# A first-FFN product placed one place earlier, two kinds of input sums formed while x arrives, and six instead of four splits of h ahead of the last silu

## The chip, the cores and the metric

The kernel runs on one core of a Trainium2 chip. TensorE multiplies, ScalarE and VectorE prepare its operands and handle its results, GpSimd and SyncE issue transfers (queues named POOL and SP in the profile). The metric is the device time of one execution in microseconds (us), median of several runs; lower is better.

## The reference

One hybrid encoder block in float32 on x of 512 tokens by 1024 features:

```
x = x + 1/2 * (silu(g1) * u1) @ W1_down,   [g1|u1] = rmsnorm(x) @ W1_gu     (5632 columns)
h = rmsnorm(x);  y = gated RG-LRU branch(h) + gated neighbourhood attention(h)
x = x + y @ W_out
x = x + 1/2 * (silu(g2) * u2) @ W2_down,   [g2|u2] = rmsnorm(x) @ W2_gu
```

The change is in the two FFNs, which share their code. Each has 22 feature tiles of 128 for its h = silu(g) * u.

## The kernel before

**Numbers in two parts.** TensorE takes operands in a reduced float32 format (`F32R`). So each operand is split into a high part H (ScalarE copies it with rounding, line 140) and a low part L (VectorE subtracts, line 143), and each matmul is done three times: high by high, low by high, high by low. In the profile the tiles are `wh`, `wl` for weights, `xh`, `xl` for x, `hh`, `hl` for h.

**Four products' worth of output from seven.** For 20 of the 22 tiles the up projection is done in five *units* of four feature tiles by `strassen`. The 512 tokens and 1024 input features are each halved, which gives x the quarters a11, a12, a22 and the sums s1, s2, s4, s3 (`FORMS`, made by `make_forms`). A unit multiplies seven of these with four weight blocks a_, b_, c_, d_ and sums of them. Each product is two halves of the contraction (`kp`) and has 24 matmuls of 128 by 512; a half needs one split weight. In unit one the order is a11, a12, s1, s2, s4, s3; the seventh, a22 (`last_product`), is done in the next unit, between s1 and s2. Results leave the banks by `evict` (ScalarE), by `plus` (VectorE adds them to an earlier result), and by `gate` and `put` (silu, scaling, a transpose, and a transfer of h to memory by `flush`). Sums of weights are made by accumulating transfers (`add`, POOL's queue) or by VectorE (`sums`).

**Sums of x.** `raw` makes the sum of one quarter pair on VectorE (lines 273 to 280), s2 from s1 and s4 from s2; `cut` rounds a pair of them to high and low parts. In the first FFN both are called when a product needs them (`need`, line 487), in the second all sums are made ahead.

**The start.** In the first FFN, x and the weights of two `plain` feature tiles arrive in eight steps; each step splits one tile of x and of the weights, squares x for the norm, keeps a scaled copy xg, and multiplies into four banks of `aux`, evicted as `pre`. In the second FFN the two plain tiles are ordinary products.

**The turn.** After the units, `finish` (line 557) fetches the turned h of unit one back (`fetch`, eight transfers on POOL's queue, four for each half of the tokens), loads three down weights and calls `ahead`, which splits h tiles by `cut`; before tile 2 it fetches unit two as well. Then `last_put` does the last silu. The down projection runs over the 22 h tiles, adding into all eight banks.

**What sets the order.** The program is written in one sequence; a planner orders each engine's instructions ahead of time. An instruction whose inputs it expects to be there goes in the order of the program, those under `high_priority` ahead of all others. Each engine then works through its list in order and waits where an input is late. Tiles carry a tag with a number of buffers: `big` 42 (sums, parts, evictions, s, h), `wh` and `wl` 4 each (split weights), `pair` 4, `PT` 5 (weights c_, d_, turned h), `wraw` 3, and 4 banks each for `acc` and `aux`. `hold` places a transfer behind a given matmul; `keep_in_program_order` fixes the order of the first loads.

Of the kernel before, what the change touches and what calls it, by code (L numbers as in the profile page):

```python
# [19 lines left out]
KT = D // P  # L20
# [19 lines left out]
C_G1, C_GM, C_G2 = 0, 8, 16  # L40
# [11 lines left out]
DFIRST = 3  # L52
# [34 lines left out]
def block_kernel(ctx: ExitStack, tc, a, out):  # L87
# [15 lines left out]
    def nm(s):  # L103
        uid[0] += 1
        return f"{s}_{uid[0]}"
# [9 lines left out]
    def acc_t():  # L115
        return acc.tile([P, T], F32, tag="acc", name=nm("acc"))

    def aux_t():
        return aux.tile([P, T], F32, tag="aux", name=nm("aux"))
# [140 lines left out]
    FORMS = "s1", "s2", "s4", "s3"  # L260
# [28 lines left out]
    def four_k(tag, bufs):  # L289
        return big.tile([P, 1024], F32, tag=tag, bufs=bufs, name=nm(tag))  # L290

    def strassen(src, units, A, norm, hd, need, ready, finish):

        half = T // 2
        prev, out, state_, rc = {}, [], {}, []

        def raws(u, i, tag, bufs):
            ts = []
            for kp in range(2):
                t = four_k(tag, bufs) if tag != "wraw" else raw_t()  # L300
                ld = nc.sync.dma_start(t, src[u, i, kp])
                if u == 0 and nld[0] < 8:
                    tc.keep_in_program_order(ld)
                ts.append(t)
            return ts

        def product(pss, ws, form, first, last, out_now=True):
            for kp in range(2):
                H, L = ws[kp]() if callable(ws[kp]) else ws[kp]
                for k2 in range(2):  # L310
                    k = kp * 2 + k2
                    c = slice(k2 * T, (k2 + 1) * T)
                    xh_, xl_ = A[form][k]
                    for tb in range(2):
                        s = slice(tb * P, (tb + 1) * P)
                        for x_, w_ in ((xh_, H), (xl_, H), (xh_, L)):
                            mark["mm"] = nc.tensor.matmul(  # L317
                                pss[tb], x_[:, s], w_[:, c], start=first and k == 0 and x_ is xh_ and w_ is H,
                                stop=k == 3 and w_ is L, skip_group_check=True)
            if out_now:  # L320
                flush()

        def operand(raw):
            w = hl_t()
            with nullcontext() if state_["u"] == 0 else tc.high_priority():
                split(raw, *w)
            return w

        def operands(ts):
            return [lambda t=t: operand(t) for t in ts]  # L330

        def add(u, ts, i):
            with tc.high_priority():
                for kp, t in enumerate(ts):
                    nc.gpsimd.dma_start(t, src[u, i, kp], accum_op=ALU.add)

        def sums(ts, os):
            def one(t, o):
                with tc.high_priority():
                    nc.vector.tensor_tensor(t, t, o, ALU.add)  # L340
                return operand(t)
            return [lambda t=t, o=o: one(t, o) for t, o in zip(ts, os)]

        def evict(pss, n):
            ts = [big_t(n=n) for _ in pss]
            with tc.high_priority():
                for t, ps in zip(ts, pss):
                    nc.scalar.activation(t, ps, AF.Copy)
            return ts

        def plus(ts, pss):
            for t, ps in zip(ts, pss):
                nc.vector.tensor_tensor(t, t, ps, ALU.add)

        def gate(ts, th):
            ss = [big_t(n="s") for _ in ts]
            for tb, (s_, t) in enumerate(zip(ss, ts)):
                j = th * 2 + tb
                nc.scalar.activation(s_, t, AF.Silu, scale=rc[0][:, j : j + 1])
            return ss  # L360

        def flush(q=nc.sync):
            while out:
                to, t2 = out.pop(0)
                hold(q.dma_start(to, t2))

        def put(u, ss, ts, th):
            for tb, (s_, t) in enumerate(zip(ss, ts)):
                j = th * 2 + tb
                mark["h"] = nc.vector.scalar_tensor_tensor(t, t, rc[0][:, j : j + 1], s_, ALU.mult, ALU.mult)  # L370
                t2 = big_t(n="ht")
                nc.vector.transpose(
                    t2.rearrange("p (c f i) -> p f c i", c=NCB, i=32), t.rearrange("p (f c i) -> p f c i", c=NCB, i=32))
                out.append((hd[u][j], t2.rearrange("p (c x) -> p c x", c=NCB)))

        def last_product(p, out_now=True):
            product(p["Z"], operands(p["a"]), "a22", False, True, out_now)

        def last_put(p):
            put(p["u"], gate(p["Z"], 1), p["u7"], 1)  # L380

        for u in range(units):
            state_["u"] = u
            a_ = raws(u, 0, "pair", 4)
            c_ = raws(u, 2, "PT", 5)
            d_ = raws(u, 1, "PT", 5)
            b_ = raws(u, 3, "wraw", 3)
            Z = [acc_t() for _ in range(2)]
            product(Z, operands(a_), "a11", True, False)
            p1 = evict(Z, "p1")  # L390
            if u == 0:
                add(u, a_, 1)
            if u == 0:
                rc.append(norm())
            if u == units - 1:
                need("plain")
            Y = [acc_t() if u == 0 else aux_t() for _ in range(2)]
            product(Y, operands(c_), "a12", True, True)
            if u == 0:
                need("s1")  # L400
            plus(p1, Y)
            if u > 0:
                s1 = gate(p1, 0)
            X = [aux_t() for _ in range(2)]
            w = operands(a_) if u == 0 else sums(a_, d_)
            product(X, w, "s1", True, False)
            add(u, d_, 3)
            p5 = evict(X, "p5")
            if prev:
                last_product(prev)  # L410
                last_put(prev)
            w = sums(a_, b_)
            if u == 0:
                need("s2")
            product(Z, w, "s2", False, False)
            add(u, a_, 2)
            u2 = evict(Z, "u2")
            if u == 0:
                need("s4")
            product(X, operands(b_), "s4", False, True)  # L420
            if u == 0:
                need("s3")
                ready(rc[0])
                s1 = gate(p1, 0)
            plus(u2, X)
            put(u, s1, u2, 0)
            product(Z, operands(d_), "s3", False, False, u < units - 1)
            plus(p5, Z)
            prev = dict(u=u, Z=Z, u7=p5, a=a_)
        last_product(prev, False)  # L430
        finish()
        last_put(prev)
        flush(nc.gpsimd)

    def ffn(wgu, ws, wd, xh, xl, forms, ssum, plain, res, emit_out, lead=None, end=None):
        units = (FT - plain) // 4
        half = T // 2
        hd = [dram.tile([NCB, P, NCB, P], F32, tag="hd", bufs=12, name=nm("hd")) for _ in range(units)]
# [27 lines left out]
        else:  # L466
            r = None
            for m in range(plain):
                pg, pu = acc_t(), acc_t()
                feat_chunk(wgu[2 * m], KT, xh, xl, pg, 0, KT)  # L470
                if r is None:
                    r, rcol, _ = rstd(ssum)
# [22 lines left out]
        def ready(rc):  # L495
# [4 lines left out]
            for tb, t in enumerate(toks):  # L500
# [8 lines left out]
        A = {"a11": quarter(0, slice(0, half)), "a12": quarter(4, slice(0, half)),  # L509
             "a22": quarter(4, slice(half, T))}  # L510
# [33 lines left out]
        def ahead(n):  # L544
            while len(cuts) < min(n, FT):
                k = len(cuts)
                if k >= plain and (k - plain) % NCB == 0:
                    u = (k - plain) // NCB
                    if u + 1 < units:
                        fetch(u + 1)  # L550
                cut(k)
# [5 lines left out]
        def finish():  # L557
            fetch(0)
            for k in first:
                ws_[k] = load_w(wd[k], 1024)  # L560
            ahead(DFIRST + 1)

        strassen(ws, units, A, norm, hd, need, ready, finish)

        def put_in(m, k, last=FT - 1):
            H, L = ws_[k]
# [92 lines left out]
    class Forms:  # L659
# [5 lines left out]

        def tile(self, k):
            self.xg.append(scaled(self.gcol, k))
            if k >= KT // 2 and self.eager:
                for n in FORMS:
                    self.raw(n, k - KT // 2)  # L670

        def cut(self, n):
            if not self.eager:
                for k in range(len(self.S[n]), len(self.S[n]) + 2):
                    self.raw(n, k)
            self.cut_(n)
# [2 lines left out]
            for n in FORMS:  # L679
                self.cut(n)  # L680

    forms = Forms(C_G1, False)

    def lead_step(k):
        square(k)
# [173 lines left out]
    A = [None] * KT  # L859
# [256 lines left out]
    for hf in range(2):  # L1116
        st = tiny.tile([P, 2, NCB, 8], F32, tag="st", name=nm("st"))
        raws = [qk_raw(0, hf, st), qk_raw(1, hf, st)]
# [42 lines left out]

    nxt = {}
    load_pairs()
    forms = Forms(C_G2, True)
    for m in range(KT):
        nc.sync.dma_start(xres[m], xd[m])
        ps = acc_t()
# [101 lines left out]
```

## Time and profile before

| | |
|---|---|
| median of 3 runs | 1106.3 us (1103.4 to 1107.08) |
| profiled execution, its own time | 1102.27 us |
| its span, first to last instruction | 1100.5 us |
| TensorE busy | 1082.4 us, 98% |
| VectorE, ScalarE, GpSimd busy | 70%, 51%, 18% |
| mean granted TensorE clock | 0.995 |

A row of the timeline has the start in us, the length in us, engine, line, operation, output<-inputs, shapes, how many instructions are merged in it, and in brackets how long the engine had been idle and what ended that. PE is TensorE, DVE VectorE, ACT ScalarE. A row of the waits has the total, how often, and the longest. A letter q behind an engine is its queue of transfers. Lines are those of the kernel before.

### The profile page before, as it was taken

What the parts mean: (1) busy time and instruction counts of PE and PEld (TensorE: products, weight loads), DVE (VectorE), ACT (ScalarE), POOL (GpSimd) and SP (SyncE); (2) the same over time, 40 slices, a digit from 0 to 9 for tenths busy, and PEclk for the clock granted to TensorE, in tenths of its full rate; (3) what the DMA queues carried; (4) which work ended last, traced back from release to release, by engine and by line L of the source; (5) the groups of instructions that cost most, each with busy time, mean ns of one, the idle gap of its engine ahead of it and who ended that gap; (6) DMA issues with size and microseconds to landing.
All of it is one profiled execution on the core that took longest, in us unless ns stands there. A gap on an engine that the chain in (4) does not pass through costs nothing. (4 is left out here: it accounts for less than half of the span.)

```text
span 1100.5 us, 14411 instructions
## 1 busy us (share of the span) xinstructions
PE 1082.4 (98%) x5121; PEld 885.4 (80%) x5121; DVE 771.3 (70%) x1222; ACT 561.6 (51%) x866; POOL 197.7 (18%) x340
## 2 busy tenths in 40 slices
PE   9899999999999999999999999999999999999998
PEld 7778888878888778788787788888888888878887
DVE  6887788774426786899878896768677887773422
ACT  7655555543314668776544543356455554543310
POOL 0101002432000333132325322000000001323000
PEclk9999999999999999999999999999999999999999
DMA  9957767785223577484679566565476777675222
GB/s 361 214 153 190 194 189 170 198 262 156 99 96 121 163 219 211 130 222 127 196 229 242 174 218 219 155 229 172 101 200 176 190 203 168 183 242 178 96 77 77
DMA packets 67463, 198.17 MB, mean 180 GB/s; under 512 B 11072, under 2 KB 12864, under 8 KB 67392
## 3 DMA queue, kind: packets, MB, share of 16 engines
q1 hardware_dynamic: 46592, 136.60, 37.4%
q0 software_dynamic: 20512, 60.34, 24.6%
q8 instruction: 40, 0.66, 0.2%
q10 hardware_dynamic: 288, 0.32, 0.1%
q14 instruction: 31, 0.25, 0.1%
HBM read 162.06 MB, written 26.74 MB: 172 GB/s over the span
## 5 line engine op out<-in xcount | busy, mean ns | idle before, releaser
L143 DVE TENSOR_TENSOR wl<-wraw,wh 128x1024 fp32r<-128x1024 f32 (+2 forms) x147 | 168.8, 1149 | 161.1 <-ACT wh L140 158.1
L140 ACT ACTIVATE wh<-wraw 128x1024 fp32r<-128x1024 f32 (+2 forms) x135 | 134.5, 998 | 225.2 <-PE acc L168 158.2
L143 DVE TENSOR_TENSOR wl<-pair,wh 128x1024 fp32r<-128x1024 f32 x80 | 97.6, 1221 | 49.4 <-ACT wh L140 49.0
L140 ACT ACTIVATE wh<-pair 128x1024 fp32r<-128x1024 f32 x80 | 84.9, 1061 | 76.7 <-PE aux L317 53.0
L167 PE MATMUL acc<-xh,wh 128*128 128x512 f32 x288 | 113.9, 396 | 0.0
L169 PE MATMUL acc<-xh,wl 128*128 128x512 f32 x288 | 112.5, 391 | 0.0
L168 PE MATMUL acc<-xl,wh 128*128 128x512 f32 x288 | 112.5, 391 | 0.0
L317 PE MATMUL acc<-wh,s 128*128 128x512 f32 x320 | 100.3, 394 | 2.9 <-ACT s L140 2.5
L317 PE MATMUL aux<-wh,s 128*128 128x512 f32 x320 | 100.3, 394 | 2.2 <-ACT s L140 2.0
L885 PE MATMUL acc<-wh,xh 128*128 128x512 f32 x192 | 75.7, 394 | 0.0
L886 PE MATMUL acc<-wh,xl 128*128 128x512 f32 x192 | 74.8, 389 | 0.0
L887 PE MATMUL acc<-wl,xh 128*128 128x512 f32 x192 | 74.7, 389 | 0.0
L317 PEld LDWEIGHTS acc<-wh,s 128*128 128x128 f32 x320 | 60.5, 190 | 17.1 <-ACT s L140 3.4
L317 PEld LDWEIGHTS aux<-wh,s 128*128 128x128 f32 x320 | 60.7, 190 | 16.1 <-ACT s L140 2.4
L168 PE MATMUL aux<-hl,wh 128*128 128x512 f32 (+1 forms) x179 | 70.1, 392 | 1.9 <-DVE hl L143 1.9
L167 PE MATMUL aux<-hh,wh 128*128 128x512 f32 (+1 forms) x179 | 68.9, 389 | 3.1 <-ACT hh L140 3.1
L169 PE MATMUL aux<-hh,wl 128*128 128x512 f32 (+1 forms) x179 | 69.8, 390 | 0.0
L317 PE MATMUL acc<-wh,xh 128*128 128x512 f32 x176 | 68.8, 391 | 0.0
L317 PE MATMUL acc<-wh,xl 128*128 128x512 f32 x176 | 68.5, 389 | 0.0
L168 PE MATMUL acc<-hl,wh 128*128 128x512 f32 (+1 forms) x176 | 68.4, 389 | 0.0
L169 PE MATMUL acc<-hh,wl 128*128 128x512 f32 (+1 forms) x176 | 68.2, 388 | 0.0
L167 PE MATMUL acc<-hh,wh 128*128 128x512 f32 (+1 forms) x176 | 68.2, 389 | 0.0
(230 smaller groups left out, 2386.7 us busy)
## 6 DMA issues: line engine op xcount, KB each, us to landing
wraw<-wqkv SPq DMA_DIRECT2D x24, 512.0 KB, 5.1
wraw<-wg SPq DMA_DIRECT2D x24, 512.0 KB, 7.1
wraw<-w1d SPq DMA_DIRECT2D x22, 512.0 KB, 3.4
wraw<-w2d SPq DMA_DIRECT2D x22, 512.0 KB, 3.4
PT<-w1s SPq DMA_DIRECT2D x20, 512.0 KB, 7.6
hT<-hd POOLq DMA_DIRECT2D x80, 128.0 KB, 3.9
PT<-w2s SPq DMA_DIRECT2D x20, 512.0 KB, 4.0
hd<-ht SPq DMA_DIRECT2D x32, 256.0 KB, 6.1
```

The source lines that it names most:

```text
L140: nc.scalar.activation(H, raw, AF.Copy)
L143: return nc.vector.tensor_tensor(L, raw, H.bitcast(F32), ALU.subtract)
L167: nc.tensor.matmul(ps, wh, xh, start=first, stop=False, skip_group_check=skip)
L168: nc.tensor.matmul(ps, wh, xl, start=False, stop=False, skip_group_check=skip)
L169: mark["mm"] = nc.tensor.matmul(ps, wl, xh, start=False, stop=last, skip_group_check=skip)
L317: mark["mm"] = nc.tensor.matmul(pss[tb], x_[:, s], w_[:, c], start=first and k == 0 and x_ is xh_ and w_ is H, stop=k == 3 and w_ is L, sk ...
L885: nc.tensor.matmul(pss[j], xh[kk][:, tj], H[:, s], start=kk == 0, stop=False)
L886: nc.tensor.matmul(pss[j], xl[kk][:, tj], H[:, s], start=False, stop=False)
L887: mark["mm"] = nc.tensor.matmul(pss[j], xh[kk][:, tj], L[:, s], start=False, stop=kk == KT - 1)
```

## The change

1. Unit two's first product (a11: its two loads, two splits, 24 matmuls and the evictions p1) is done by `begin` in the first FFN between unit one's products s1 and s2. Unit two later takes it up where it would have begun.
2. `Forms` takes a list of forms that are made as x arrives; the first FFN gives s1 and s2, the second all four as before.
3. In the first FFN, weight splits and weight sums of units one and two have the program's order; before, this held for the splits of unit one alone, in both FFNs. In the second FFN, the splits of unit one have priority now.
4. The bank pair Y of a unit's second product is always from `aux`.
5. `finish` calls `ahead` for six h tiles instead of four, with priority; the fetch of unit two's h lies inside it.

```diff
-    def strassen(src, units, A, norm, hd, need, ready, finish):
+    def strassen(src, units, A, norm, hd, need, ready, finish, early):
...
         def operand(raw):
             w = hl_t()
-            with nullcontext() if state_["u"] == 0 else tc.high_priority():
+            with nullcontext() if state_["u"] < 2 and early else tc.high_priority():
                 split(raw, *w)
             return w
...
             def one(t, o):
-                with tc.high_priority():
+                with nullcontext() if state_["u"] < 2 and early else tc.high_priority():
                     nc.vector.tensor_tensor(t, t, o, ALU.add)
                 return operand(t)
...
+        def begin(u):
+            a_ = raws(u, 0, "pair", 4)
+            Z = [acc_t() for _ in range(2)]
+            product(Z, operands(a_), "a11", True, False)
+            return a_, Z, evict(Z, "p1")
+
+        begun = {}
         for u in range(units):
             state_["u"] = u
-            a_ = raws(u, 0, "pair", 4)
+            a_, Z, p1 = begun.pop(u) if u in begun else begin(u)
             c_ = raws(u, 2, "PT", 5)
             d_ = raws(u, 1, "PT", 5)
             b_ = raws(u, 3, "wraw", 3)
-            Z = [acc_t() for _ in range(2)]
-            product(Z, operands(a_), "a11", True, False)
-            p1 = evict(Z, "p1")
...
-            Y = [acc_t() if u == 0 else aux_t() for _ in range(2)]
+            Y = [aux_t() for _ in range(2)]
...
             p5 = evict(X, "p5")
+            if u == 0 and early:
+                begun[1] = begin(1)
             if prev:
...
-            ahead(DFIRST + 1)
+            with tc.high_priority():
+                ahead(DFIRST + 3)
...
         def tile(self, k):
             self.xg.append(scaled(self.gcol, k))
-            if k >= KT // 2 and self.eager:
-                for n in FORMS:
+            if k >= KT // 2:
+                for n in self.eager:
                     self.raw(n, k - KT // 2)

         def cut(self, n):
-            if not self.eager:
+            if n not in self.eager:
...
-    forms = Forms(C_G1, False)
+    forms = Forms(C_G1, ("s1", "s2"))
...
-    forms = Forms(C_G2, True)
+    forms = Forms(C_G2, FORMS)
```

`early` is true in the first FFN only.

More of the change, by code (lines that the diff above doesn't have):

```diff
@@ L560, in finish @@
                 ws_[k] = load_w(wd[k], 1024)
-            ahead(DFIRST + 1)
-        strassen(ws, units, A, norm, hd, need, ready, finish)
+            with tc.high_priority():
+                ahead(DFIRST + 3)
+        strassen(ws, units, A, norm, hd, need, ready, finish, lead is not None)
         def put_in(m, k, last=FT - 1):
```

## The prediction

> **What bounds the kernel now.** I read the page's busy shares first, then TensorE's waits (up to 200 us and behind it), then the stretches around those waits (us, then each engine's busy time and instructions, the granted clock, the DMA share), and then each engine in order of time.
>
> ```profile
> span 1100.5 us, 14411 instructions
> PE 1082.4 (98%) x5121; PEld 885.4 (80%) x5121; DVE 771.3 (70%) x1222; ACT 561.6 (51%) x866; POOL 197.7 (18%) x340
> ...
> PE acc L317 <- ACT s L140: 2.5, 1, 2.5
> PE aux L317 <- ACT s L140: 2.0, 1, 2.0
> ...
> PE aux L167 <- ACT hh L140: 3.1, 2, 1.5
> ...
> 92.00:240.00 148.00, 147.96 (x653) 122.02 (x651) 113.65 (x129) 76.61 (x95) 29.05 (x44) 1.00 0.74 201
> ...
> 45.14:76.49 31.35, 26.37 (x97) 0.89 0.72 176
> 223.37:246.50 23.13, 20.56 (x83) 0.93 0.77 261
> 968.63:989.44 20.81, 18.36 (x79) 1.00 0.69 228
> ```
>
> TensorE is the bound: busy for 98%, and without a gap from 92 to 240 us, where 147.96 / 653 = 0.2266 us is one matmul at full pace. A change gains only where it waits. The stretch from 45.14 to 76.49 holds four products of 24 matmuls, unit one's s2, s4 and s3 and unit two's first: 96 x 0.2266 = 21.8, so 9.6 us are lost. In the other two, the turns from the units to the down projection, 83 and 78 matmuls (18.8 and 17.7 us) leave 4.3 and 3.1 us lost. These 17 us are the most that the change can win.
>
> **How the first loss arises.**
>
> ```profile
> 42.07 0.94 PE L317 MATMUL aux<-wh,s 128*128 128x512 f32 x2
> 47.84 0.80 PE L317 MATMUL acc<-wh,s 128*128 128x512 f32 x2 [2.54 <-ACT s L140]
> 48.92 0.80 PE L317 MATMUL acc<-wh,s 128*128 128x512 f32 x1 [0.28 <-DVE s L143]
> 49.94 0.63 PE L317 MATMUL acc<-wh,s 128*128 128x512 f32 x1
> 50.37 0.63 PE L317 MATMUL acc<-wl,s 128*128 128x512 f32 x1
> 57.53 1.48 PE L317 MATMUL aux<-wh,s 128*128 128x512 f32 x3 [1.97 <-ACT s L140]
> 65.13 0.73 PE L317 MATMUL acc<-wh,s 128*128 128x512 f32 x2
> ...
> 45.20 1.04 ACT L140 ACTIVATE wh<-wraw 128x1024 fp32r<-128x1024 f32 x1
> 46.15 0.58 ACT L348 ACTIVATE p<-aux 128x512 f32<-128x512 f32 x1
> 47.16 0.63 ACT L140 ACTIVATE s<-s 128x512 fp32r<-128x512 f32 x1 [0.43 <-DVE s L256]
> ...
> 36.14 0.69 DVE L143 TENSOR_TENSOR s<-s,s 128x512 fp32r<-128x512 f32 x1
> 37.87 0.75 DVE L258 TENSOR_TENSOR s<-xg,xg 128x256 f32<-128x256 f32 x2
> 46.38 0.75 DVE L256 SCALAR_TENSOR_TENSOR s<-s,xg 128x256 f32<-128x256 f32 x2
> ```
>
> A result lands 0.16 after the next matmul could start (0.39 long, 0.23 apart), so s1's product ends its issue at 47.84 - 2.54 - 0.16 = 45.14, and TensorE's gap ahead of s2 is 2.70. In it ScalarE splits the second weight of b (45.20), evicts s1's second half (46.15), waits 0.43 for VectorE's sum (begun at 46.38) and only then rounds s2's first half (47.16). The gap ahead of s4, 55.40 to 57.53, is 2.13 by the same working. After each, matmuls start 0.43 us apart (49.94, 50.37), half pace: s2 takes 7.56 us up to 55.40 and s4 7.60 up to 65.13, against 5.44 each, so 2.1 and 2.2, with s2's wait of 0.28 in the first.
>
> Why are s2's sums so late? They need only s1's sums, done by 38.6. Yet they start right behind the eviction p5 (46.15), whose tile the program makes just ahead of theirs; and s1's second pair of sums (37.87) starts only behind its first low part (36.14), whose tile also comes first. I read this as an order: tiles of one tag are first written as the program makes them.
>
> **The change in the first FFN's front.** Unit two's first product now stands between s1 and s2. It brings two loads, two splits on ScalarE and VectorE, 24 matmuls and two evictions.
>
> ```profile
> L143 DVE TENSOR_TENSOR wl<-pair,wh 128x1024 fp32r<-128x1024 f32 x80 | 97.6, 1221 | 49.4 <-ACT wh L140 49.0
> 16.98 4.86 SPq L301 DMA_DIRECT2D pair<-w1s  x2
> 20.54 0.68 DVE L143 TENSOR_TENSOR wl<-wraw,wh 128x512 fp32r<-128x512 f32 x1
> ```
>
> The loads were SP's next ones already, issued by 21.8, so neither SP's order nor POOL's changes ahead of s2. The splits (1.04 and 1.22 each) have until 45, and the sums that leave VectorE's busy stretch ahead of it (four pairs of 0.75) make room for its 2.4. The 24 matmuls then cover 5.44 us, 45.1 to 50.6. But the new evictions stand ahead of s2's halves in the order of tiles, as p5 did, and with four weight buffers in turn b's second split again comes free at the end of the product just before s2. So split, eviction and rounding follow one another once more, and the gap moves rather than goes: 2.70 less the 0.43 for the sums; of that I take 0.29, as the wait on VectorE gave other work a little room. The 0.28 goes, because no sums stand ahead of the low part. **Gain 0.57.** Bounds: 0, and 2.70 + 2.12 = 4.82 if the halves are cut while the moved product runs, so that neither the gap nor its slow start is left. I stay near the low end, as p5 ahead of s2 is the nearest row.
>
> s4 keeps its gap and slow start behind u2's evictions: **0** (bounds -1, VectorE late by one split for it, and 4.3, both gone).
>
> At 42.07 two matmuls take 0.94 instead of 0.23 + 0.39, waiting for s1's second low part, which was late by its own sums: **0.32**. From 65.13 to 76.49 48 matmuls take 11.36 instead of 10.88, s3 and the product that now moves away being mixed there: **0.48** (bounds 0.48 and -2: nothing fills s3 any more if its halves are late; they have the 7.6 us of s4 to be made in).
>
> The sums of s1 and s2 made as x arrives are 8 operations of 0.34 (half of a pair's 0.75, overlapped) in the last four steps, 0.67 a step. The last split of x's steps starts at 20.54 and may move by three steps' worth, 2.0, to 22.5 and end at 23.2; TensorE reaches that step at 27.5 - 12 x 0.2266 = 24.8. **0**, hidden under the matmuls of the steps before; without that cover it would be up to 2.0. Unit one's and two's additions and unit two's splits lose their priority on VectorE and ScalarE: behind a late one stands its product, which has a product's 5.4 us before it: **0**, bounds -1 and 1. Y in aux: no bank appears among what TensorE waits for: **0**. In the second FFN unit one's splits gain priority, ahead of sums that TensorE doesn't wait for either: **0**, bounds -1 and 0.
>
> The front gives 0.57 + 0.32 + 0.48 = 1.4.
>
> **The change at the turn.**
>
> ```profile
> 238.66 1.06 ACT L140 ACTIVATE wh<-wraw 128x1024 fp32r<-128x1024 f32 x1 [5.06 <-PE acc L168]
> 239.63 0.40 ACT L140 ACTIVATE hh<-hT 128x256 fp32r<-128x256 f32 x1
> 240.02 1.06 ACT L140 ACTIVATE wh<-wraw 128x1024 fp32r<-128x1024 f32 x1
> 240.98 1.62 ACT L140 ACTIVATE hh<-hT 128x256 fp32r<-128x256 f32 x5
> ...
> 242.25 0.42 DVE L143 TENSOR_TENSOR hl<-hT,hh 128x256 fp32r<-128x256 f32 x1
> 242.66 1.76 DVE L143 TENSOR_TENSOR hl<-hT,hh 128x256 fp32r<-128x256 f32 x5
> ...
> 241.74 0.73 PE L167 MATMUL aux<-hh,wh 128*128 128x512 f32 x2 [1.53 <-ACT hh L140]
> 243.47 0.79 PE L168 MATMUL aux<-hl,wh 128*128 128x512 f32 x1 [0.99 <-DVE hl L143]
> ...
> 987.26 2.09 DVE L143 TENSOR_TENSOR hl<-hT,hh 128x256 fp32r<-128x256 f32 x6
> 988.40 0.50 PE L168 MATMUL aux<-hl,wh 128*128 128x512 f32 x1 [0.92 <-DVE hl L143]
> ```
>
> TensorE's start at 241.74 fits the second of five halves (ends 241.69) and 243.47 the third low part (242.66 + 0.33 + 0.42 = 243.41). I read it so: the first token half of the fifth and sixth h tile goes ahead of the second token half of the third, which TensorE needs. The edit puts six tiles, not four, ahead of the last silu, so those two leave this place. The needed low part then ends first, at 242.67, not 243.41: **0.74**. In the second FFN it ends two of six (2 x 0.33) sooner: **0.67**. It still comes behind the weight splits, the first of which waits until 238.66 for its buffer. Bounds: 4.3 + 3.1, both token halves ahead and no wait, and -5.6 (first rival).
>
> **Sum.** 1.4 + 0.74 + 0.67 = 2.8. The profiled execution took 1102.27 (its span and 1.77 around it), which gives 1099.5. The runs' median is 1106.3, 4.0 above the profiled one; taken from there the forecast is 1106.3 - 2.8 = **1103.5**.
>
> [...]
>
> **Rivals.**
>
> ```profile
> 201.65 0.94 POOL L335 DMA_DIRECT2D pair<-w1s  x1 [10.23 <-DVE wl L143]
> 204.93 0.90 POOL L528 DMA_DIRECT2D hp<-hp  x1
> 242.62 1.28 ACT L713 ACT_TABLE_LOAD   x1
> 244.79 0.17 DVE L715 TENSOR_SCALAR z<-ex 128x16 f32<-128x16 f32 x1
> 248.95 0.18 DVE L723 TENSOR_TENSOR pol<-pol,z 128x16 f32<-128x16 f32 x1
> ```
>
> Slower: **unit two's fetch overtakes.** Its eight transfers now have priority and can pass three of unit one's second token half on POOL, as the accumulating load (201.65) passed the last of hp's eight. An order that counts on that half late puts the LRU's constants ahead of it: ScalarE's table and exponential (1.28 + 0.22) from 240.98, a hand-over (0.25), then VectorE's chain, nineteen operations of which take 4.2 above, so 5.3 for all 24; the low part ends at 248.4 instead of 243.41, 4.9 later, with 0.7 more of half pace. -1.4 - 0.67 + 5.6 = +3.5: 1109.8. It decides once the second half stands behind the table load. Against it: the constants must find that gap.
>
> **s2's halves are cut early**: 4.82 + 0.32 + 0.48 + 1.4 = 7.0, 1099.3; VectorE's room speaks for it, p5 against. **Both token halves go ahead of the silu**: 1.4 + 4.3 + 3.1 = 8.8, 1097.5; they would have to land before 232. **Short gaps keep the clock**: 2.8 + 4.0 (1.84 + 2.16 of slow starts) = 6.8, 1099.5; the second FFN's turn kept 1.00, the front's 0.89 speaks against. **The planner undoes the move**, hoisting other matmuls: 1106.3.
>
> **How the numbers follow.** Forecast 0.34, overtaking 0.24, early cuts 0.18, both halves 0.13, the clock 0.06, undone 0.05. The range, 1095 to 1110.5, holds two gains together at one end and the slower case at the other; the forecast's own is 1101 to 1106. A measurement of this kernel tells about 0.3% (3.3 us) from no change. Faster: the three large gains (0.37) and a quarter of the forecast, 0.46. Slower: half of the overtaking and some of the rest, 0.18. The same: 0.36.
>
> **What would show it.** Right: a gap of 2 to 2.5 us moved to near 50.5, with an eviction of p just ahead of s2's first half; s4's gap unchanged; no half of h between the two weight splits at 240. The overtaking: a table load ahead of the needed half. Wrong: s2's first half ahead of unit two's evictions, or a turn without a wait.

## The result

| | before | after |
|---|---|---|
| median | 1104.42 us (6 runs, 1100.62 to 1107.08) | 1115.13 us (6 runs, 1114.11 to 1115.54) |
| ratio | | 1.0095, 95% interval 1.0075 to 1.0115 |
| profiled execution, its span | 1100.5 us | 1113.4 us |

The changed kernel is slower by about 10.5 us; the forecast was 1103.5 us and the range ended at 1110.5. Among the kernels below, two executions far out, 1216.49 us of constants late (its profiled one, granted clock 0.846) and 5131.27 us of early sums only, are left out of all ratios and losses.

First three stretches of each kernel (from and to in us, length, then busy time and instructions of TensorE, its weight loads, VectorE, ScalarE and GpSimd, then granted clock, DMA share, GB/s): the front of the first FFN, its turn, and the turn of the second. The kernel before:

```profile
38.00:80.00 42.00, 36.97 (x143) 28.12 (x142) 37.11 (x56) 24.47 (x34) 3.45 (x4) 0.92 0.76 196
225.00:262.00 37.00, 34.47 (x145) 27.76 (x145) 22.07 (x59) 14.99 (x28) 12.69 (x22) 0.95 0.69 225
955.00:1025.00 70.00, 67.55 (x296) 55.14 (x295) 38.90 (x61) 28.71 (x50) 21.98 (x38) 1.00 0.68 211
```

The changed kernel:

```profile
38.00:80.00 42.00, 36.83 (x151) 28.81 (x150) 34.73 (x52) 24.66 (x34) 3.45 (x4) 0.96 0.82 210
225.00:262.00 37.00, 27.68 (x109) 21.96 (x108) 21.06 (x57) 13.13 (x27) 12.68 (x22) 0.86 0.68 209
955.00:1025.00 70.00, 65.60 (x278) 53.23 (x277) 40.07 (x60) 30.69 (x51) 27.20 (x46) 0.95 0.73 211
```

With 0.2266 us for a matmul at full pace, a stretch loses its length less 0.2266 times its matmuls. The front goes from 42 - 143 x 0.2266 = 9.60 to 7.78, the first turn from 4.14 to 12.30, the second from 2.93 to 7.01. So the front gained 1.8 and the turns lost 8.2 + 4.1 = 12.2. The spans differ by 12.9. Most of what is left over is the start: s1's first matmul comes at 41.55 instead of 39.35, as TensorE's first matmuls ran at a slower pace in this execution (three took 1.62 us from 5.88 on, where they took 0.93 from 5.65 on before); the runs below show that this does not come from the early sums.

**The first turn after.** ScalarE, then VectorE, then TensorE in the timeline of the changed kernel:

```profile
239.13 1.06 ACT L140 ACTIVATE wh<-wraw 128x1024 fp32r<-128x1024 f32 x1 [3.28 <-PE acc L168]
240.21 1.28 ACT L720 ACT_TABLE_LOAD   x1
241.50 0.22 ACT L720 ACTIVATE ex<-ab 128x16 f32<-128x16 f32 x1
241.62 1.04 ACT L140 ACTIVATE wh<-wraw 128x1024 fp32r<-128x1024 f32 x1
242.57 3.77 ACT L140 ACTIVATE hh<-hT 128x256 fp32r<-128x256 f32 x12
...
244.04 0.42 DVE L143 TENSOR_TENSOR hl<-hT,hh 128x256 fp32r<-128x256 f32 x1
245.28 0.42 DVE L143 TENSOR_TENSOR hl<-hT,hh 128x256 fp32r<-128x256 f32 x1
248.79 0.17 DVE L739 TENSOR_SCALAR sn<-sp 128x16 f32<-128x16 f32 x1
248.91 2.77 DVE L143 TENSOR_TENSOR hl<-hT,hh 128x256 fp32r<-128x256 f32 x8
...
245.47 0.73 PE L167 MATMUL aux<-hh,wh 128*128 128x512 f32 x1 [4.80 <-ACT hh L140]
250.73 0.80 PE L168 MATMUL aux<-hl,wh 128*128 128x512 f32 x1 [4.53 <-DVE hl L143]
255.59 0.50 PE L167 MATMUL aux<-hh,wh 128*128 128x512 f32 x1
```

The table load now stands between the two weight splits, and behind them come twelve halves of h in a row (before: one and five). TensorE starts at 245.47. Twelve halves of 0.40 that start 0.306 apart put the end of the ninth at 242.57 + 8 x 0.306 + 0.40 = 245.42. So TensorE waited for the ninth. On VectorE four halves (the first at 244.04, the fourth at 245.28) alternate with the constants, the chain runs to 248.9, and of the eight behind it the fifth ends at 248.91 + 4 x 0.336 + 0.42 = 250.67; TensorE goes on at 250.73, at half pace (starts 0.43 us apart, not 0.23) up to 255.59.

Whose halves are the eight in front? The order that the planner wrote for GpSimd's queue, with unit one's and unit two's transfers of h:

```
before: unit one, first half x4; unit one, second half x4; unit two x8
after:  unit one, first half x4; unit one, second half x1; unit two x8; unit one, second half x3
```

and its order for ScalarE behind the second weight split: four first halves of unit two, four second halves of unit two, and only then the four second halves of unit one. TensorE's next tile, the third, is unit one's.

**The second turn after** has no constants, and the same twelve:

```profile
994.70 3.77 ACT L140 ACTIVATE hh<-hT 128x256 fp32r<-128x256 f32 x12
995.96 4.10 DVE L143 TENSOR_TENSOR hl<-hT,hh 128x256 fp32r<-128x256 f32 x12
...
997.60 0.79 PE L167 MATMUL aux<-hh,wh 128*128 128x512 f32 x1 [3.68 <-ACT hh L140]
999.11 0.80 PE L168 MATMUL aux<-hl,wh 128*128 128x512 f32 x1 [0.72 <-DVE hl L143]
```

Again TensorE starts when the ninth is done (994.70 + 8 x 0.306 + 0.40 = 997.55).

**The front after**, ScalarE and TensorE:

```profile
51.95 0.60 ACT L348 ACTIVATE p<-acc 128x512 f32<-128x512 f32 x1 [1.20 <-PE acc L317]
52.45 1.05 ACT L140 ACTIVATE wh<-wraw 128x1024 fp32r<-128x1024 f32 x1
53.39 0.59 ACT L348 ACTIVATE p<-acc 128x512 f32<-128x512 f32 x1
53.87 1.15 ACT L140 ACTIVATE s<-s 128x512 fp32r<-128x512 f32 x2
...
54.55 0.73 PE L317 MATMUL acc<-wh,s 128*128 128x512 f32 x2 [1.96 <-ACT s L140]
56.41 0.50 PE L317 MATMUL acc<-wh,s 128*128 128x512 f32 x1 [1.13 <-DVE s L143]
63.65 1.54 PE L317 MATMUL aux<-wh,s 128*128 128x512 f32 x3 [1.96 <-ACT s L140]
```

The gap ahead of s2 has moved behind unit two's first product, with an eviction, the split of b and an eviction ahead of the rounding of s2's halves (53.87). The gap ahead of s4 (63.65) has stayed.

### The profile page after: what moved, and what is told of

Same layout as the page of the kernel before. It is cut to its first block, busy times and chain, and to the rows that moved or that the text cites. A ratio compares the mean times of both kernels' runs of the same rounds, so it can differ in the third digit from the quotient of the medians.

```text
span 1113.4 us, 14401 instructions
## 1 busy us (share of the span) xinstructions
PE 1086.3 (98%) x5121; PEld 888.7 (80%) x5121; DVE 770.7 (69%) x1222; ACT 562.0 (50%) x866; POOL 197.7 (18%) x340
## 5 line engine op out<-in xcount | busy, mean ns | idle before, releaser
L892 PE MATMUL acc<-wh,xh 128*128 128x512 f32 x192 | 75.7, 394 | 0.0
L893 PE MATMUL acc<-wh,xl 128*128 128x512 f32 x192 | 74.8, 389 | 0.0
L140 ACT ACTIVATE wh<-PT 128x1024 fp32r<-128x1024 f32 x40 | 42.3, 1060 | 44.9 <-PE acc L317 35.8
L167 PEld LDWEIGHTS acc<-xh,wh 128*128 128x128 f32 x288 | 54.1, 188 | 13.0 <-issue 2.3
```

The lines of the kernel that those rows point to most:

```text
L140: nc.scalar.activation(H, raw, AF.Copy)
L167: nc.tensor.matmul(ps, wh, xh, start=first, stop=False, skip_group_check=skip)
L892: nc.tensor.matmul(pss[j], xh[kk][:, tj], H[:, s], start=kk == 0, stop=False)
L893: nc.tensor.matmul(pss[j], xl[kk][:, tj], H[:, s], start=False, stop=False)
```

## The experiments

Times are medians; each ratio is to the kernel before on the same chip, with its 95% interval. The losses are those of the three stretches, from each kernel's profile; counts at the edges make them uncertain by about 0.4, and a stretch without a wait gives -0.4 to 0.1. Each row is from one profile; that of constants late is from its second run.

| kernel | us | ratio | front | turn 1 | turn 2 |
|---|---|---|---|---|---|
| before | 1104.4 to 1105.6 | 1 | 9.60 | 4.14 | 2.93 |
| after | 1115.13 | 1.0095 [1.0075, 1.0115] | 7.78 | 12.30 | 7.01 |
| turn only | 1114.96 | 1.0084 [1.0064, 1.0105] | 9.60 | 11.62 | 7.01 |
| front only | 1102.73 | 0.9972 [0.9958, 0.9986] | 7.78 | 2.78 | 4.51 |
| moved product only | 1104.44 | 1.0007 [0.9988, 1.0025] | 8.92 | 2.78 | 5.65 |
| early sums only | 1104.88 | 0.9991 [0.9973, 1.0009] | 9.82 | 4.60 | 4.06 |
| constants late | 1110.70 | 1.0054 [1.0031, 1.0077] | 9.14 | 8.00 | 6.78 |
| unit one's fetch with priority | 1104.05 | 0.9996 [0.9976, 1.0015] | 8.46 | 2.78 | 6.10 |
| six tiles, no priority | 1099.27 | 0.9939 [0.9920, 0.9958] | 8.46 | 1.88 | 1.57 |
| s2's halves early | 1098.78 | 0.9948 [0.9928, 0.9969] | 5.29 | 1.42 | 1.57 |
| unit one's halves first | 1094.97 | 0.9927 [0.9900, 0.9954] | 8.69 | -0.39 | -0.25 |
| both of these | 1096.37 | 0.9931 [0.9905, 0.9957] | 8.46 | 0.06 | -0.25 |
| turn alone, mended | 1097.10 | 0.9926 [0.9899, 0.9953] | 9.82 | 0.06 | -0.25 |

### Which part loses

Turn only: the kernel before with

```diff
-            ahead(DFIRST + 1)
+            with tc.high_priority():
+                ahead(DFIRST + 3)
```

> The kernel before with the turn's edit alone (six tiles of h cut ahead instead of four, and all with priority). Theory, from the traces: unit two's fetch gets priority with the cuts and passes three of the four pieces of unit one's second token half on GpSimd's queue; in the first FFN the exp table's load and the constants on VectorE, and in both FFNs the eight halves of unit two's tiles, then stand ahead of unit one's second halves. From the changed kernel's profile the turn of the first FFN costs 68.48 - 59.95 - 2 matmuls of 0.2266 = 8.1 us more than before and that of the second 64.10 - 60.00 = 4.1, so +12.2, about 1116.6. The rival as the prediction priced it (the constants alone, in the first FFN alone, the other turn as forecast) expects +3.5 us; the forecast expected a gain of 1.4 us. If the loss came from the front and not from the turns, this kernel is within 0.3% of before.

It measures 1114.96, the whole loss, and its two turns lose nearly what those of the changed kernel lose. The rival's +3.5, the forecast's gain at the turns and a loss in the front all fall.

Front only: the changed kernel with these lines undone.

> The changed kernel with the turn put back (four tiles cut ahead, no priority); the moved product and the two eager sums stay. The two profiles give -1.8 us for the front itself (37.14 to 35.32 from s1's first matmul to the a12 product) and +2.2 us for the time up to s1 (39.35 to 41.55). If the 2.2 belong to the eager sums, the kernel is at before + 0.4 and TensorE starts s1 near 41.5; if TensorE's slow first 4 us were chance of that one execution, s1 starts near 39.4 and the kernel is at before - 1.8. The prediction's front term was -1.4. With the front to blame for the whole loss it would stand at before + 10.

1102.73 us, ratio 0.9972: a gain of 1.5 to 4.6 us. The front's loss is that of the changed kernel (7.78). What of the start? These are the first three matmuls and s1's first of front only, of turn only (no early sums), and of "unit one's halves first", a kernel from below that has the early sums:

```profile
5.64 1.62 PE L465 MATMUL aux<-wh,xh 128*128 128x512 f32 x3 [0.79 <-ACT xh L191]
40.97 0.62 PE L317 MATMUL aux<-wh,s 128*128 128x512 f32 x2
```

```profile
5.58 1.62 PE L459 MATMUL aux<-wh,xh 128*128 128x512 f32 x3 [0.73 <-DVE wh L450]
41.07 0.62 PE L317 MATMUL aux<-wh,s 128*128 128x512 f32 x2
```

```profile
5.57 0.93 PE L465 MATMUL aux<-wh,xh 128*128 128x512 f32 x3 [0.73 <-DVE wh L456]
39.28 0.61 PE L317 MATMUL aux<-wh,s 128*128 128x512 f32 x2
```

The slow start (1.62 for three, not 0.93) comes without the early sums too, and turn only then reaches s1 at 41.07, as late as front only with them (40.97). After a quick start the early sums cost nothing either: s1 at 39.28, against 39.35 in the kernel before. So the 2.2 us go with the pace of TensorE's first matmuls and not with the edit, and the sums in the lead are hidden.

### Count, priority, or the fetch

Six tiles, no priority: the changed kernel with

```diff
-            with tc.high_priority():
-                ahead(DFIRST + 3)
+            ahead(DFIRST + 3)
```

> The changed kernel with six tiles cut ahead, but without the priority. Theory: without priority the fetches keep their order on GpSimd's queue, unit one's second halves come straight behind the two weight splits, ahead of the table load and of unit two's halves, with two first halves fewer ahead of them than before: the turn's wait shortens from 3.1 to about 2.4 us in the first FFN, a gain near 0.7 each as the prediction's turn terms had it, so about 1.4 us below the kernel with the front alone. If the count of six and not the priority made the loss, it is about 12 us above it.

1099.27, 3.5 below front only, more than the 1.4 expected, and about 0.6% below the kernel before (ratio 0.9939). GpSimd's order is that of before, unit one's second halves come straight behind the weight splits, and TensorE's two waits in each turn (1.53 and 0.99; 1.53 and 0.92) are one:

```profile
242.67 0.73 PE L167 MATMUL aux<-hh,wh 128*128 128x512 f32 x2 [1.23 <-ACT hh L140]
243.24 0.63 PE L167 MATMUL acc<-hh,wh 128*128 128x512 f32 x2
985.47 0.73 PE L167 MATMUL aux<-hh,wh 128*128 128x512 f32 x2 [1.23 <-ACT hh L140]
```

The waits shrink by 1.29 and 1.22, and the pace behind them is full (starts 0.23 us apart from 244.29 and from 987.09 on). The wait for ScalarE loses 0.30, the time of one half. That for VectorE goes: its halves come earlier, and TensorE's list now has two more matmuls that need only hh (243.24) ahead of the first that needs hl. The count was good, the priority was not.

Unit one's fetch with priority: the changed kernel with

```diff
-            fetch(0)
+            with tc.high_priority():
+                fetch(0)
```

> The changed kernel with unit one's fetch inside the priority too, so that it cannot be passed by unit two's. The exp table's load and a part of the constants still stand ahead of unit one's second halves in the first FFN, unit two's eight halves no longer do. Theory: ScalarE's rounding of the first needed half ends at 242.6 + 0.4 = 243.0 instead of 245.4, its low part at 244.0 + 0.4 = 244.4 instead of 250.6; in the second FFN 995.1 and 996.4. Of the 12.2 us about 11 come back: within 0.3% of before. If the constants were the main cause, only the second FFN's 4.1 come back and it stays 8 us above before.

1104.05, 11 us below the changed kernel, as expected. In the first turn the halves of unit one are the first of the eight behind the weight split, and TensorE starts with them:

```profile
243.30 2.55 ACT L140 ACTIVATE hh<-hT 128x256 fp32r<-128x256 f32 x8
243.75 0.74 PE L167 MATMUL aux<-hh,wh 128*128 128x512 f32 x2 [2.35 <-ACT hh L140]
```

With the changed kernel's priority kept and the order on the queue restored, the first turn loses 2.78 instead of 12.30, although the table load still stands ahead (hence 2.35, not 1.23).

The second turn does not do what was expected. The two fetches, now of equal priority, alternate on the queue there, and ScalarE still has twelve halves in a row:

```profile
985.06 3.77 ACT L140 ACTIVATE hh<-hT 128x256 fp32r<-128x256 f32 x12
986.74 0.80 PE L167 MATMUL aux<-hh,wh 128*128 128x512 f32 x1 [2.45 <-ACT hh L140]
988.15 0.80 PE L168 MATMUL aux<-hl,wh 128*128 128x512 f32 x1 [0.61 <-DVE hl L143]
```

TensorE starts when the fifth is done (985.06 + 4 x 0.306 + 0.40 = 986.68), so four of unit two's halves still stand ahead, and the turn loses 6.10, part of it by half pace (starts 0.43 us apart up to 993.01). This gives the overtaking in three steps: in the second turn TensorE waits for ScalarE 1.23 us with none of unit two's halves ahead (six tiles, no priority), 2.45 with four and 3.68 with eight. Each four cost 1.22 or 1.23, which is 4 x 0.306. So the overtaking is the cause. Priority for the splits with unit two's fetch left out of it was not tried.

Constants late: the changed kernel with

```diff
-    after(nc.vector.tensor_scalar(nlam, lam, -1.0, None, ALU.mult), mark["h"])
+    after(nc.vector.tensor_scalar(nlam, lam, -1.0, None, ALU.mult), mark["mm"])
```

> The changed kernel, in which the constants' first operation (nlam) is ordered behind the first FFN's last matmul instead of behind the last h; unit two's fetch and halves still pass unit one's. If the constants alone made the first turn's loss (the rival as the prediction priced it), the first turn falls from 12.3 us lost to about 4 and the kernel to about 1107. If unit two's eight halves cost it by themselves, the first turn looks like the second, which has no constants (7.0 us lost): ScalarE's ninth half ends at about 244.0, VectorE's at about 245.5 instead of 250.6, so about 5 us come back and the kernel is near 1110. If the foreign halves alone made all of it, it stays at 1115.

1109.88 us (ratio 1.0052, 1.0033 to 1.0072). The same kernel ran once more for a profile of its turn:

> The changed kernel with the constants behind the first FFN, once more, for a profile of its first turn. By the time it showed first (ratio 1.0052 to before, where the changed kernel has 1.0095) about 5 of the changed kernel's 12 us are the constants', the rest unit two's halves. In that case TensorE waits about 3.7 us for hh and 0.7 for hl in the first turn, as in the second (3.68 and 0.72), where the changed kernel has 4.80 and 4.53, and the first turn loses about 7 us instead of 12.3.

```profile
243.39 3.77 ACT L140 ACTIVATE hh<-hT 128x256 fp32r<-128x256 f32 x12
...
246.30 0.50 PE L167 MATMUL aux<-hh,wh 128*128 128x512 f32 x1 [3.68 <-ACT hh L140]
247.81 0.80 PE L168 MATMUL aux<-hl,wh 128*128 128x512 f32 x1 [1.02 <-DVE hl L143]
```

1110.70, and the first turn now looks like the second: the wait for hh is the expected 3.68, that for hl 1.02 where 0.7 was expected. It loses 8.00 instead of 12.30. So behind unit two's halves the constants cost 4.3 us. The turns are then 8.00 - 4.14 = 3.9 and 7.01 - 2.93 = 4.1 worse than before, which is what unit two's eight halves cost less what the six tiles gain.

### The front's two parts

Moved product only is front only with no form made early (`Forms(C_G1, ())`); early sums only is the kernel before with `Forms(C_G1, ("s1", "s2"))`.

> The kernel before with unit two's first product between s1 and s2 alone: no sum is made as x arrives, and the turn is as before. By the prediction's terms: 0.57 for the gap ahead of s2 (part of it the sums' share) and 0.48 for s3 that is no longer mixed with another product: about -1, the front's loss from 9.6 to about 8.6. If the front's gain needs the eager sums, nothing (9.6).

> The kernel before with the sums of s1 and s2 made as x arrives alone. By the prediction's terms: 0.32 for the stall inside s1, 0.43 of VectorE's share in the gap ahead of s2 and 0.28 for its low part: about -1, and s1 starts no later than in other executions whose first matmuls ran at 1.62 (41 to 41.7). If the sums in the lead are not hidden, s1 starts up to 2.0 us later than that.

Neither differs from before. Ahead of s2, with the product moved alone:

```profile
53.62 1.87 PE L317 MATMUL acc<-wh,s 128*128 128x512 f32 x3 [3.08 <-ACT s L140]
```

and with the early sums alone:

```profile
48.91 0.73 PE L317 MATMUL acc<-wh,s 128*128 128x512 f32 x2 [1.97 <-ACT s L140]
51.03 0.79 PE L317 MATMUL acc<-wh,s 128*128 128x512 f32 x1 [1.39 <-DVE s L143]
```

Without the early sums ScalarE is 3.08 late at the new place. With them and without the move, what ScalarE gains is lost again at VectorE's low part. In both, as in the changed kernel, about 3 us of waits are left ahead of s2, and only their place and split change (2.54 + 0.28 before, 1.96 + 1.13 after). The gain of both together beside nothing from each is larger than these waits explain, and its cause is not shown; a part of it is pace, below.

### Better versions

s2's halves early: six tiles without priority, and `need("s2")` ahead of unit two's first product instead of behind it.

> The kernel with six tiles cut ahead without priority, in which the halves of s2's sums are also made in the program ahead of unit two's first product and not behind its evictions. The prediction said that the gap ahead of s2 only moves because tiles of one tag are first written in program order, so that the halves stand behind the evictions. If that is right, ScalarE rounds them during s1 or the moved product, TensorE's wait of 1.96 us for ScalarE and 1.8 for VectorE ahead of s2 and the slow pace behind it go, and the front's loss falls from 8.5 to about 4.5 (s4's gap stays): about -3 to -4 against the kernel with six tiles cut ahead. If it is the split of b's weight or the wh buffers that set the start of s2, nothing changes.

TensorE has no wait ahead of s2 any more, and the front's loss falls to 5.29: the halves' place in the program did hold them back, and not b's weight. Whether it did so by the order of the tiles or by the order of the instructions, which the edit both changes, is not told apart. But s4 then waits twice:

```profile
60.26 1.36 PE L317 MATMUL aux<-wh,s 128*128 128x512 f32 x3 [1.96 <-ACT s L140]
66.66 0.50 PE L317 MATMUL aux<-wh,s 128*128 128x512 f32 x1 [1.16 <-DVE s L143]
...
64.78 1.23 DVE L340 TENSOR_TENSOR pair<-pair,PT 128x1024 f32<-128x1024 f32 x1 [3.04 <-DMA PT<-w1s]
```

VectorE reached a sum of weights (64.78) whose transfer had not landed, and s4's second low part stood behind it. The time, 1098.78, can't be told from that of the kernel without this edit: of the 3.2 us that the front gains, the spans of the two profiles show 1.0 (1098.4 and 1097.4). What took the rest is open.

Unit one's halves first: six tiles without priority, the down projection's fifth and sixth weight split ordered behind unit one's last second half, and the constants behind that too.

```diff
             ws_[k] = load_w(wd[k], 1024)
+            if k in (DFIRST + 1, DFIRST + 2):
+                after(mark["act"], mark["t1"])
...
-    after(nc.vector.tensor_scalar(nlam, lam, -1.0, None, ALU.mult), mark["h"])
+    after(nc.vector.tensor_scalar(nlam, lam, -1.0, None, ALU.mult), mark["t1"])
```

(`mark["act"]` is the latest high part of a split, `mark["t1"]` that of unit one's last second half.)

> The kernel with six tiles cut ahead without priority, in which the two weight splits that stood ahead of unit one's second halves (the down projection's fifth and sixth tile) are ordered behind them. Theory: those splits wait for TensorE to give back weight buffers (ScalarE idle 3.2 us ahead of the first of them) while the halves' data has long landed, so the halves are late only by their place. ScalarE rounds them right behind the silu, near 236.7, VectorE takes them near 239.5, and TensorE waits in neither turn: the losses of 1.88 and 1.57 us go, about -3 against the kernel with six tiles. If the second halves' data were late, or the two weight splits become the next wait (they are then done 1.3 to 2 us later, near 243.5, and TensorE needs the fourth and fifth weight at 250), less or nothing is gained.

```profile
225.00:262.00 37.00, 37.00 (x165) 30.63 (x164) 22.10 (x60) 16.07 (x29) 12.69 (x22) 1.00 0.87 239
955.00:1025.00 70.00, 70.00 (x310) 57.79 (x309) 38.81 (x62) 28.50 (x52) 18.40 (x32) 1.00 0.65 198
...
232.18 1.25 ACT L359 ACTIVATE s<-acc,rcol 128x512 f32<-128x512 f32 x2
233.32 1.33 ACT L140 ACTIVATE hh<-hT 128x256 fp32r<-128x256 f32 x4
237.78 1.06 ACT L140 ACTIVATE wh<-wraw 128x1024 fp32r<-128x1024 f32 x1 [3.14 <-PE acc L168]
```

In these two rows, the turns, TensorE waits in neither (busy for 37.00 of 37.00 and 70.00 of 70.00). ScalarE takes unit one's second halves straight after the silu, at 233.32, without a wait for their transfer, in the time in which it otherwise waited for a weight buffer (3.14 of it are still idle). 1094.97 us, 9.7 below the kernel before beside it: the best kernel here.

> Both of the last two edits: s2's halves made ahead of unit two's first product, and unit one's second halves ahead of the weight splits. If the two gains are separate places on the path, they add: about 6 to 7 us below the kernel with six tiles, near 1093.

1096.37: the gains don't add. s4's wait for VectorE is 2.83 here, and the front loses 8.46 as without the edit of s2.

The last run is the mended turn on the old front: the kernel before with six tiles, without priority, and the same two orders.

> The kernel before with six tiles cut ahead without priority and unit one's second halves ordered ahead of the down projection's fifth and sixth weight split, and the constants behind these halves; the front as before. Theory: both of before's waits in the turns go (4.1 and 2.9 us lost), so about -7 us against before, and the rest of the gain of the kernel with all three edits (-9.7) is the front's. If the turn needs the changed front (the later or earlier arrival of TensorE), it gains less.

1097.10, ratio 0.9926: 8.5 us where 7 were expected, and by the ratios the same as with the changed front (0.9927). What the front adds beside a mended turn stays open.

## Why the prediction was wrong

**The turn's terms, +0.74 and +0.67, failed.** The step was: "The edit puts six tiles, not four, ahead of the last silu, so those two leave this place. The needed low part then ends first, at 242.67". The reading of the row behind it (a third low part behind two halves of the fifth and sixth tile) was right: with the count alone the two waits shrink by 1.29 and 1.22, more than was forecast, in part because TensorE's own order changed too. But the edit has a second half, the priority, and inside it lies unit two's fetch. The sum put that at nothing and left it to a rival with a chance of 0.24. It moved the needed halves themselves: in the first turn TensorE got them at 245.4 and 250.7, not at 241.7 and 242.7, and the two turns lost 8.2 and 4.1 us where 0.74 and 0.67 were to be gained.

**The slower rival named the mechanism and undersized it** (1109.8 written, 1115.13 measured). The fetch passes three of unit one's four transfers on GpSimd's queue, and the table load and the chain go ahead of the needed half, as written. Its 5.6 us for the constants measured 4.3. Of its terms, the hand-over of 0.25 is 0.03 in the traces (before, the exponential starts at 244.54 and is 0.22 long, z starts at 244.79), and the 0.7 of half pace was an estimate: behind the wait for hl, matmuls took 1.4 more than at full pace before (243.47 to 246.50) and 2.4 more after (250.73 to 255.59). What its price lacked was the other work of that gap: unit two's eight halves, whose data comes earlier on the queue, 3.9 us net in the first turn. For the same reason the second turn did not keep its gain of 0.67 but lost 4.1, although it has no constants. 4.3 + 3.9 + 4.1 = 12.3, not 5.6 - 0.67 in the two turns. The doubt set against it, "the constants must find that gap", did not hold: in the trace after the table load (240.21) and twelve halves stand there.

**The front's 1.4 came near by luck, not by its terms.** The front alone gained 1.5 to 4.6 us. The losses of the six profiles with the changed front and the old place of s2's halves (7.78 twice, 8.46 twice, 8.69, 9.14) are 0.5 to 1.8 below the 9.60 of before. The gap ahead of s2 moved behind the evictions of p, as written, and the halves do follow these because of their place in the program (they went ahead when made earlier); that it is the order of the tiles is argued, not shown. But the 0.57 was not won: ScalarE's part fell from 2.54 to 1.96, and VectorE's, to go from 0.28 to nothing, rose to 1.13, behind the low part of b. The two together are no shorter, 3.09 against 2.82. The stall in s1 went (0.32 as priced). s3 takes 76.87 - 71.23 = 5.64 unmixed, and the moved product 5.44: 11.08 instead of 11.36, 0.28 where 0.48 was priced. What made up for the missing 0.57 is pace, which the sum did not have. Besides its wait, s2 takes 6.98 - 1.13 = 5.85 us, where it took 7.56 - 0.28 = 7.28 before: it runs at full pace from 56.41 on (0.50 long), where it began at half pace before (48.92, 0.80). So 0.32 + 0.28 + 1.43 less the 0.27 of longer waits is 1.76, the front's 1.8. In the profiles of front only, six tiles without priority and unit one's fetch with priority it is s4 that starts at nearly full pace (0.54 to 0.58 us over 5.44, where before lost 2.16), and s2 loses 2.0 to 3.2 by pace. So one of the two slow starts has gone each time; why is not shown.

**The zeros.** The sums in the lead: right, s1 starts at about the same time with and without them in executions that start alike. s4's gap: right, 1.97 and 1.96; its slow start stayed in the changed kernel's profile, and not in those three profiles. Y, and the priorities in the units: no wait of TensorE's in the trace after comes from them.

**The other rivals.** "Both token halves go ahead of the silu" comes close to what the mended turn does, with the second halves right behind the silu: 1097.5 was written, 1094.97 and 1097.10 were measured. Their data has landed by 233.3; whether by 232, the rival's condition, is not shown. "s2's halves are cut early" was priced at 4.82 for the gap alone; the front's loss fell by 3.2, as s4 took a part of it over. "The planner undoes the move" fell, as s2 follows the moved product (54.55), and so did "short gaps keep the clock", as three matmuls of s4 take 1.54 behind a wait of 1.96 (63.65).

## What to carry to other kernels

Priority belongs to everything inside the block, transfers too: before giving it to a step, list what the step issues on each queue, what older work still stands there, and every consumer that becomes ready earlier. Where a needed operation is late only by its place behind one that waits for a buffer, an explicit order of the two removes the wait (here 1.23 us in each turn), and a priority may not. Two edits in one step are to be sized apart: here the count gained 3.5 us, and the priority on top of it lost 16.

## What the hardware did that was not expected

The same code with the same waits runs on at full pace in one kernel and at half pace in another. The second turn is the same in the kernel before and with the product moved alone, and TensorE has the same two waits in it, 1.53 and 0.92 us. Ten microseconds around them, of the kernel before and then with the product moved alone, and the first matmul behind the second wait in the latter (0.50 long in the kernel before, quoted in the prediction):

```profile
985.00:995.00 10.00, 7.55 (x32) 5.77 (x32) 4.63 (x9) 4.11 (x10) 4.63 (x8) 1.00 0.70 209
985.00:995.00 10.00, 7.55 (x20) 5.33 (x19) 4.46 (x8) 3.10 (x8) 4.24 (x8) 0.66 0.79 205
988.88 0.79 PE L168 MATMUL aux<-hl,wh 128*128 128x512 f32 x1 [0.92 <-DVE hl L143]
```

TensorE is busy for 7.55 us in both, but with 32 matmuls at a granted clock of 1.00 in one and 20 at 0.66 in the other. Front only and early sums only have these two waits as well, and behind the second their matmuls stay at half pace for 3.4 and 2.7 us, with the product moved alone for 5.7. The turn loses 2.93, 5.65, 4.51 and 4.06 in the four. So the half pace behind the same waits costs from nothing to 2.7 us, and nothing in the turn's code decides which.

The runs of one kernel vary in the same way. Beside "unit one's halves first", the kernel before took 1100.03 us at a mean granted clock of 0.998 and 1106.79 at 0.992, and 0.6% of 1100 is 6.6. Its spread was 8 us (1100.8 to 1109.0 in 23 runs), that of the kernel with six tiles and no priority 2.3 (1097.8 to 1100.2 in 6). The number of waits does not settle it: the three kernels without a wait in either turn spread over 5.0, 5.2 and 5.6. In the front and in the slower rival the prediction charged the half pace with every gap.

The waits ahead of the half pace are short: 1.53 and 0.92 us in these rows, and a single one of 1.97 (57.53, in the prediction). What decides when the clock falls, no run shows.
